# Stage edges of a two-layer decoder step on one Trainium2 core: alpha rows ordered later, meta keys in the values' tile, one PSUM division, the last beta by transfers

## The chip, the core and the metric

The kernel runs on one core of a Trainium2 chip. The metric is the device time of one execution in microseconds; of several runs the median counts. The engines are named as the profile names them: PE (TensorE, matmuls; PEld is its weight load), DVE (VectorE), ACT (ScalarE), POOL (GpSimd) and SP (SyncE, which here only issues DMAs). Each engine works through its own queue in order. DMAs issued by SP and by POOL go to the core's 16 DMA engines.

## The reference

One inference step of a decoder trunk with two layers, for a prompt of 1024 tokens behind 16 meta tokens and for 8 samples of one token with 4096 tokens of past each. Width 1024, 8 heads of 128 in layer 1, 4096 hidden units, all in float32.

```python
for layer in range(2):
    if layer == 0:
        f_p, st_p = gla_prompt(x_p, ...)          # gated linear attention in chunks of 64
        f_s, st_s = gla_sample(x_s, state_gla, ...)
    else:
        f_p, kp_rows, vp_rows = diff_prompt(x_p, ...)
        f_s, ks_rows, vs_rows = diff_sample(x_s, cache_k, cache_v, page_table, ...)
    x_p = post_norm(x_p, f_p, ln_mix_g[layer], ln_mix_b[layer])
    x_s = post_norm(x_s, f_s, ln_mix_g[layer], ln_mix_b[layer])
    x_p = post_norm(x_p, sq_relu_mlp(x_p, w1[layer], w2[layer]), ln_mlp_g[layer], ln_mlp_b[layer])
    x_s = post_norm(x_s, sq_relu_mlp(x_s, w1[layer], w2[layer]), ln_mlp_g[layer], ln_mlp_b[layer])
y_prompt = x_p[:, 16:]

def post_norm(x, f, g, b):   # DeepNorm: layer_norm(ALPHA * x + f) * g + b, ALPHA = 4 ** 0.25
    return layer_norm(ALPHA * x + f, g, b)

def diff_core(q, k, v, q_pos, k_pos, lam):
    s = einsum('bqhmd,bkhmd->bhmqk', q, k) * 64 ** -0.5   # m = 0, 1: two score maps per head
    p = softmax(where(k_pos <= q_pos, s, -inf))
    return einsum('bhqk,bkhe->bqhe', p[:, :, 0] - lam * p[:, :, 1], v)
```

The samples' attention runs over 256 pages (128 tokens, 8 heads, 128 values) of keys and as many of values, gathered by a page table: 512 KB each. The outputs are the prompt's and the samples' rows, the GLA states, and the new key and value rows of both.

## The kernel before

Weights and activations are each split into a high part and a low part, and a product is three matmuls: `mm3` (L195 to L197) multiplies high by high, high by low and low by high. `unit` loads weights in pieces (`raw`), ACT writes the high part `whi` (L182), POOL the low part `wlo` (L183). The pool `wsp` holds two buffers of each, of 2048 columns. The activations stand feature-major in `XH` and `XL`; `Y` (`Yt`, row-major, 8 tiles of 128 tokens) holds the residual stream, in which each layer's output is added up.

The stages follow each other on PE: GLA to about 480 us, its output product to 680, the MLP of layer 0 to 1436, the QKV projection to 1791, attention from 1800 to 2068, its output product (`w_out`), and from 2200 the MLP of layer 1, in 4 groups `g` of 7 up and 7 down steps `i` with operands that are sums and differences of blocks (`mlp1`, `weight_operand`, `chip_operand`). The decode of the samples (`decode`) runs beside the MLP of layer 0 and the QKV projection: SP loads pages (`pg`, L739), DVE and POOL multiply keys (L770), DVE sums (L771), PE multiplies values (L811) and turns the result (L825).

The order within an engine's queue is not written by hand throughout: a scheduler builds it from a simulated timeline, in which dependences, the buffers of pools and the banks of PSUM decide what may go when. `tc.issue_after(x)` holds the instructions written under it back behind instruction x.

- `normalize` is the LayerNorm that closes a stage: row statistics (L904, L908), the power -0.5 on POOL (L913), scale and shift on ACT, then `to_fm`, which turns the rows (PE, L930) and applies gain and shift. What the next residual needs of them is added to `Y` by `alpha_row`: L951 multiplies `Y` by the gain row times ALPHA, L953 adds the shift row times ALPHA; the rows come as tiles `ht` by DMA (L946).
- In the QKV projection, after unit u=3 `alpha_row` is written for `ln_mlp_g`, after u=6 for `ln_mlp_b`, with the four stores of the residual to `xres` (L1065). Each tile's rope is L1049 to L1052 on DVE, its stores L1058.
- Attention: `prep(h)` loads the keys and queries of a head into a tile of name `wlo` (L1101, L1102), the 16 meta tokens' keys into `km` (L1103, pool `a2`, 4 buffers, which opens once the decode pool is closed), their values into `vm`, the values into a tile of name `whi` (L1105). PE turns `km` (L1113), the keys (L1118) and the queries (L1123); POOL's DMAs move halves between partitions (L1129 to L1135), for all heads but the first. `tile_` makes scores (L1153 to L1155 for head 0, L1157 and L1158 for the others), the softmax, the transposes of the probabilities (L1176) and the product with the values (PV, L1181). `o_norm` normalises two heads at a time on POOL (L1192, L1193); `o_fm` turns the outputs for `w_out` (L1199). `prep(h + 1)` is written at the start of head h.
- PSUM has 8 banks. `psum(mm=3, ax=3, sm=2)` opens three pools; after attention `psum(mm=4, ax=2, sm=2)` closes them and opens others.
- The end: the rows of a finished tile pass `normalize`, and `last` multiplies by the gain (L1311) and adds the shift on POOL (L1314), or, for tiles 2 and 3, does both on DVE (L1319, L1320); SP stores them (L1315, L1321). `samples_out` brings the samples' sums from two PSUM banks (`acc`, filled by small products beside the weights in `beside`, L1416), turns them (L1334), normalises (`s_ln`, L470 to L491) and turns them back (L1343); before, it is written after step i=4 of the last group, whose down steps run in the order 1, 5, 6, 7, 4, 3, 2.

## Time and profile before

| | |
|---|---|
| median of 3 runs | 2927.53 us (2924.68 to 2937.85) |
| profiled execution | 2915.81 us |
| its span | 2914.1 us |
| PE busy | 2783.9 us, 96% |
| DVE busy | 1857.9 us, 64% |
| POOL busy | 1145.4 us, 39% |
| ACT busy | 1038.3 us, 36% |
| moved by DMA | 643.83 MB, mean 221 GB/s |

The span reaches from the first to the last instruction of the profiled execution; its time contains a little more. Busy times are sums over the span. PE is never short of work for long, so what is to be read is where its busy time within a stretch is below the stretch's length, where its clock is below 1.00, and what it waited for there.

### The profile page before, as it was taken

The numbers are of one execution on the slowest core, as the hardware profiler recorded it, in microseconds if no ns is written. First come the engines' busy times: TensorE is split into PE (matmuls) and PEld (weight loads), VectorE is DVE, ScalarE is ACT, GpSimd is POOL, SyncE is SP. The second block draws the span as 40 slices with busy tenths as digits, with TensorE's granted clock in tenths as the row PEclk, the third lists the DMA queues.
The fourth block names the chain that finished last, engine by engine and source line by source line (L and its number), as shares of the span: only waits on it lengthen the run. The fifth ranks groups of instructions, "written<-read, shape, count | busy, mean of one in ns | idle before, by whom it ended". The sixth has DMA issues, their size and how long they took to land. (4 is left out here: it accounts for less than half of the span.)

```text
span 2914.1 us, 52192 instructions
## 1 busy us (share of the span) xinstructions
PE 2783.9 (96%) x19668; PEld 2275.1 (78%) x19668; DVE 1857.9 (64%) x2976; ACT 1038.3 (36%) x2071; POOL 1145.4 (39%) x885
## 2 busy tenths in 40 slices
PE   8999999999999999999989999989898999999996
PEld 5776668987777777777888986878788889797985
DVE  2664544458877877777676731878438755838378
ACT  2343354151122122122411111777325535345343
POOL 1321122234333333433323430122326766677666
PEclk9999999999999999999999998999899999999998
DMA  8667541524798888988488988463427878796972
GB/s 262 210 214 248 187 168 39 191 73 164 255 341 309 309 328 310 331 315 321 137 274 288 360 298 260 102 135 84 116 98 214 230 224 234 195 288 163 270 205 86
DMA packets 299308, 643.83 MB, mean 221 GB/s; under 512 B 35168, under 2 KB 150880, under 8 KB 287792
## 3 DMA queue, kind: packets, MB, share of 16 engines
q1 hardware_dynamic: 267520, 531.15, 52.8%
q0 software_dynamic: 31536, 109.35, 15.2%
q8 instruction: 155, 2.54, 0.3%
q14 instruction: 97, 0.79, 0.1%
HBM read 582.89 MB, written 40.91 MB: 214 GB/s over the span
## 5 line engine op out<-in xcount | busy, mean ns | idle before, releaser
L183 POOL TENSOR_TENSOR wlo<-raw,whi 128x512 fp32r<-128x512 f32 x256 | 361.2, 1425 | 786.0 <-ACT whi L182 697.6
L195 PE MATMUL mmt<-whi,XH 128*128 128x256 f32 (+1 forms) x1824 | 554.0, 305 | 7.5 <-DVE qr L1051 3.8
L196 PE MATMUL mmt<-wlo,XH 128*128 128x256 f32 (+1 forms) x1824 | 550.8, 303 | 0.5 <-POOL wlo L183 0.5
L195 PE MATMUL mmt<-XH,whi 128*128 128x512 f32 (+1 forms) x1376 | 480.1, 350 | 15.7 <-DVE HL L192 6.4
L197 PE MATMUL mmt<-XH,wlo 128*128 128x512 f32 (+1 forms) x1376 | 479.4, 350 | 0.0
L197 PE MATMUL mmt<-whi,XL 128*128 128x256 f32 x1536 | 440.5, 287 | 6.8 <-DVE XL L192 6.8
L195 PEld LDWEIGHTS mmt<-whi,XH 128*128 128x128 f32 x1824 | 346.3, 190 | 43.6 <-issue 19.8
L182 ACT CAST whi<-raw 128x512 fp32r<-128x512 f32 x256 | 152.4, 619 | 619.0 <-PE mmt L197 247.3
L196 PEld LDWEIGHTS mmt<-wlo,XH 128*128 128x128 f32 x1824 | 346.6, 190 | 25.0 <-issue 11.7
L771 DVE TENSOR_REDUCE sc<-pg 128x16 f32<-128x1024 f32 x256 | 309.6, 1214 | 78.4 <-POOL pg L770 74.9
L197 PEld LDWEIGHTS mmt<-whi,XL 128*128 128x128 f32 x1536 | 292.3, 190 | 22.7 <-issue 14.8
L196 PE MATMUL mmt<-XL,whi 128*128 128x512 f32 x768 | 307.6, 400 | 0.0
L195 PEld LDWEIGHTS mmt<-XH,whi 128*128 128x128 f32 x1376 | 261.2, 190 | 57.5 <-DVE HL L192 8.2
L770 DVE TENSOR_TENSOR pg<-pg,qb 128x1024 f32<-128x1024 f32 x192 | 261.3, 1366 | 59.1 <-DMA pg<-in_cache_k 42.9
L197 PEld LDWEIGHTS mmt<-XH,wlo 128*128 128x128 f32 x1376 | 261.2, 190 | 43.6 <-issue 12.0
L770 POOL TENSOR_TENSOR pg<-pg,qb 128x1024 f32<-128x1024 f32 x64 | 156.3, 2443 | 286.3 <-DMA pg<-in_cache_k 215.0
L195 PE MATMUL mmt<-whi,HH 128*128 128x512 f32 x512 | 205.3, 401 | 1.4 <-DVE Y L995 1.4
L196 PE MATMUL mmt<-wlo,HH 128*128 128x512 f32 x512 | 204.5, 399 | 0.0
L197 PE MATMUL mmt<-whi,HL 128*128 128x512 f32 x512 | 203.7, 398 | 0.0
L196 PEld LDWEIGHTS mmt<-XL,whi 128*128 128x128 f32 x768 | 145.2, 189 | 40.4 <-issue 8.9
L196 PE MATMUL mmt<-XH,whi 128*128 128x258 f32 x608 | 173.0, 286 | 3.7 <-DMA XH<-xc 2.9
L1397 POOL TENSOR_TENSOR wlo<-RW,whi 128x512 fp32r<-128x512 f32 x96 | 152.4, 1678 | 56.6 <-ACT whi L1396 56.5
(432 smaller groups left out, 5482.1 us busy)
## 6 DMA issues: line engine op xcount, KB each, us to landing
pg<-in_cache_k SPq DMA_DIRECT2D x256, 512.0 KB
pg<-in_cache_v SPq DMA_DIRECT2D x256, 512.0 KB
XH<-xc POOLq DMA_DIRECT2D x42, 1032.0 KB, 8.8
raw<-in_mlp_w SPq DMA_DIRECT2D x164, 256.0 KB
rw<-in_mlp_w SPq DMA_DIRECT2D x156, 256.0 KB
swt<-in_mlp_w SPq DMA_DIRECT2D x32, 1024.0 KB
RW<-in_mlp_w POOLq DMA_DIRECT2D x96, 256.0 KB, 7.3
xc<-XH POOLq DMA_DIRECT2D x14, 1032.0 KB, 8.0
```

Of the source, the lines that this page charges most:

```text
L182: S.copy(hi[:, c], raw)
L183: G.tensor_tensor(lo[:, c], raw, hi[:, c].bitcast(F32), op=ALU.subtract)
L195: TE.matmul(ps, ah, bh, start=first, stop=False)
L196: TE.matmul(ps, ah, bl, start=False, stop=False)
L197: TE.matmul(ps, al, bh, start=False, stop=last)
L770: eng.tensor_tensor(pg, pg, qb, op=ALU.mult)
L771: return V.tensor_reduce(sc[:, n, :], pg.rearrange("p (h d) -> p h d", d=64), op=ALU.add, axis=AX.X).ins
L1397: G.tensor_tensor(lo[:, k, :], t, hi[:, k, :].bitcast(F32), op=ALU.subtract)
```

## The change

Five edits, in the order of the program.

1. The three PSUM pools are opened once, with 3, 3 and 2 banks, and stay. The tiles of `mlp1` take a bank of `ax` at every other tile instead of every third.
2. The `alpha_row`s of layer 0's second norm are held behind the last step of DVE that the program has recorded so far (`steps_v[-1]`): the rope of the unit they are written after. Their loads and the stores to `xres` follow them.
3. `km` is no tile of its own; the meta tokens' keys lie in columns 1024 to 1151 of the values' tile `whi`.
4. The last norm's shift is written into `y_prompt` beforehand, by one transfer from DRAM to DRAM that repeats the row `ln_mlp_b[1]` 1024 times; the finished rows, with the gain alone, are added to it by POOL's accumulating transfers. For tiles 2 and 3 ACT multiplies by the row's scale. Only the gain row is held on the chip.
5. In the last group, the samples' loads that stood beside four operands (i=5, 6, 7, 4) all stand beside two (i=5 and 6), and `samples_out` is written after i=6.

```diff
-    psum(mm=3, ax=3, sm=2)
+    mm = ctx.enter_context(tc.tile_pool(name="mm", bufs=3, space=PSUM))
+    ax = ctx.enter_context(tc.tile_pool(name="ax", bufs=3, space=PSUM))
+    sm = ctx.enter_context(tc.tile_pool(name="sm", bufs=2, space=PSUM))
...
         if u == 3:
-            list(alpha_row(A["ln_mlp_g"][0:1], ALU.mult))
+            with tc.issue_after(steps_v[-1]):
+                list(alpha_row(A["ln_mlp_g"][0:1], ALU.mult))
         elif u == 6:
-            for j in alpha_row(A["ln_mlp_b"][0:1], ALU.add):
-                cs = slice(256 * j, 256 * j + 256)
-                dma(A["xres"][:, cs].rearrange("(t p) n -> p t n", p=P), Yt[:, :, cs])
+            with tc.issue_after(steps_v[-1]):
+                for j in alpha_row(A["ln_mlp_b"][0:1], ALU.add):
+                    cs = slice(256 * j, 256 * j + 256)
+                    dma(A["xres"][:, cs].rearrange("(t p) n -> p t n", p=P), Yt[:, :, cs])
...
-        km, vm = a2.tile([NM, P], F32, name="km"), vms[h % 2]
+        km, vm = vk[:NM, 1024 : 1024 + P], vms[h % 2]
...
-    psum(mm=4, ax=2, sm=2)
...
-    fgb = [XF[1][:, 1024 * i : 1024 * (i + 1)] for i in range(2)]
+    fg = XF[1][:, :1024]
...
-        y = Yt[:, t, :]
+        y, out = Yt[:, t, :], A["y_prompt"][0, t * P : (t + 1) * P, :]
         if t not in (2, 3):
-            V.tensor_tensor(y, y, fgb[0], op=ALU.mult)
-            for h in range(4):
-                c = slice(256 * h, 256 * h + 256)
-                G.tensor_tensor(y[:, c], y[:, c], fgb[1][:, c], op=ALU.add)
-            dma(A["y_prompt"][0, t * P : (t + 1) * P, :], y)
+            V.tensor_tensor(y, y, fg, op=ALU.mult)
+            nc.gpsimd.dma_start(out, y, accum_op=ALU.add)
             return
         for h in range(2):
             c = slice(512 * h, 512 * h + 512)
-            V.scalar_tensor_tensor(y[:, c], y[:, c], mv[:, t, 0:1], fgb[0][:, c], ALU.subtract, ALU.mult)
-            V.scalar_tensor_tensor(y[:, c], y[:, c], rs[:, 0, t : t + 1], fgb[1][:, c], ALU.mult, ALU.add)
-            dma(A["y_prompt"][0, t * P : (t + 1) * P, c], y[:, c])
+            V.scalar_tensor_tensor(y[:, c], y[:, c], mv[:, t, 0:1], fg[:, c], ALU.subtract, ALU.mult)
+            S.activation(y[:, c], y[:, c], AF.Copy, scale=rs[:, 0, t : t + 1])
+            nc.gpsimd.dma_start(out[:, c], y[:, c], accum_op=ALU.add)
...
-        beside.quarter = {5: (0, 0), 6: (1, 1), 7: (0, 1), 4: (1, 0)}.get(i)
+        quarters = {5: [(0, 0), (1, 0)], 6: [(0, 1), (1, 1)]} if g == 3 else {5: [(0, 0)], 6: [(1, 1)], 7: [(0, 1)], 4: [(1, 0)]}
...
-                down_tile(g, i, t, *now, axt() if n % 3 == 0 else mmt())
+                down_tile(g, i, t, *now, axt() if n % 2 else mmt())
...
-            if g == 3 and not up and i == 4:
+            if g == 3 and not up and i == 6:
                 samples_out()
...
-                for x, nm in zip(fgb, "gb"):
-                    dma(x, A["ln_mlp_" + nm][1:2].broadcast_to([P, D]))
+                dma(fg, A["ln_mlp_g"][1:2].broadcast_to([P, D]))
+                dma(A["y_prompt"][0], A["ln_mlp_b"][1:2].broadcast_to([T, D]))
```

What the scheduler makes of it is seen in the queues. The lines of the changed kernel are 7 to 9 lower than those of the kernel before (L811 is L802 there, L1113 is L1106, L1153 is L1146, L1176 is L1169, L1181 is L1174, L1199 is L1192, L195 is L186).

PE's queue at the start of attention, before: `pg` are the last pages of values, `km` and `wlo` the first heads' meta keys, keys and queries, `XH_83` and `XL_85` head 0's operands.

```order
L197 MATMUL mmt<-whi,XL_86 128x256
L811 MATMUL smt<-pg,sc 16x256 x12
L825 MATMUL smt<-c_ident,pg 128x128 x2
L1113 MATMUL axt<-c_ident,km 128x16
L1118 MATMUL axt<-c_ident,wlo 128x128 x4
L1123 MATMUL axt<-c_ident,wlo 128x128 x4
L1118 MATMUL axt<-c_ident,wlo 128x128 x4
L1123 MATMUL axt<-c_ident,wlo 128x128 x4
L1113 MATMUL axt<-c_ident,km 128x16
L1153 MATMUL mmt<-XH_83 128x352
L1154 MATMUL mmt<-XL_85,XH_83 128x352
L1153 MATMUL mmt<-XH_83 128x352
```

The same place in the changed kernel; the meta keys are read from `whi`:

```order
L188 MATMUL mmt<-whi,XL_86 128x256
L1106 MATMUL axt<-c_ident,whi 128x16
L1111 MATMUL axt<-c_ident,wlo 128x128 x4
L802 MATMUL smt<-pg,sc 16x256 x4
L1116 MATMUL axt<-c_ident,wlo 128x128 x4
L802 MATMUL smt<-pg,sc 16x256 x4
L1111 MATMUL axt<-c_ident,wlo 128x128 x4
L802 MATMUL smt<-pg,sc 16x256 x4
L1116 MATMUL axt<-c_ident,wlo 128x128 x4
L802 MATMUL smt<-pg,sc 16x256 x4
L1146 MATMUL mmt<-XH_83 128x352
L1147 MATMUL mmt<-XL_85,XH_83 128x352
```

The preparation of head 0 moved in front of the last pages, between single ones, and so did head 0's first score products; 16 more page matmuls, head 1's preparation and the last 32 page matmuls follow them.

PE's queue within a head in the middle of attention, before (`XH_83`, `XL_85`: the operands of the head whose scores are made; `vm_21001` and `whi` behind L1181: the values of the head before it; `km` and `wlo`: the next head's rows):

```order
L1157 MATMUL mmt<-XH_83 128x384
L1158 MATMUL mmt<-XH_83,XL_85 128x384
L1176 MATMUL axt<-c_ident,as 128x128 x4
L1113 MATMUL axt<-c_ident,km 128x16
L1118 MATMUL axt<-c_ident,wlo 128x128 x4
L1157 MATMUL mmt<-XH_83 128x400
L1158 MATMUL mmt<-XH_83,XL_85 128x400
L1157 MATMUL mmt<-XH_83 128x384
L1158 MATMUL mmt<-XH_83,XL_85 128x384
L1181 MATMUL smt<-vm_21001,aT 128x128
L1181 MATMUL smt<-whi,aT 128x128 x3
L1123 MATMUL axt<-c_ident,wlo 128x128 x4
```

The same head in the changed kernel:

```order
L1174 MATMUL smt<-vm_21001,aT 128x128
L1174 MATMUL smt<-whi,aT 128x128 x3
L1150 MATMUL mmt<-XH_83 128x384
L1151 MATMUL mmt<-XH_83,XL_85 128x384
L1150 MATMUL mmt<-XH_83 128x400
L1151 MATMUL mmt<-XH_83,XL_85 128x400
L1150 MATMUL mmt<-XH_83 128x384
L1151 MATMUL mmt<-XH_83,XL_85 128x384
L1106 MATMUL axt<-c_ident,whi 128x16
L1111 MATMUL axt<-c_ident,wlo 128x128 x4
L1116 MATMUL axt<-c_ident,wlo 128x128 x4
```

The transpose of the meta keys moved from two score pairs ahead of the last PV products to three score pairs behind them.

PE's queue at the end of attention, before; `Y` holds the heads' outputs, `XH_83` and `XL_85` now their feature-major parts, and L195 to L197 are `w_out`:

```order
L1199 MATMUL axt<-c_ident,Y 128x128 x4
L1181 MATMUL smt<-vm_21001,aT 128x128
L1181 MATMUL smt<-whi,aT 128x128 x3
L1199 MATMUL axt<-c_ident,Y 128x128 x4
L1181 MATMUL smt<-whi,aT 128x128 x2
L1199 MATMUL axt<-c_ident,Y 128x128 x24
L1285 MATMUL smt<-zoq,one 128x64
L195 MATMUL mmt<-whi,XH_83 128x256
L196 MATMUL mmt<-wlo,XH_83 128x256
```

The changed kernel where its first product of `w_out` stands; behind the last row shown, further ones stand among the last heads' L1169 and L1174:

```order
L1192 MATMUL axt<-c_ident,Y 128x128 x4
L1150 MATMUL mmt<-XH_84 128x336
L1151 MATMUL mmt<-XH_84,XL_86 128x336
L1150 MATMUL mmt<-XH_84 128x320
L1151 MATMUL mmt<-XH_84,XL_86 128x320
L1192 MATMUL axt<-c_ident,Y 128x128 x4
L186 MATMUL mmt<-whi,XH_83 128x256
L187 MATMUL mmt<-wlo,XH_83 128x256
L188 MATMUL mmt<-whi,XL_85 128x256
L186 MATMUL mmt<-whi,XH_83 128x256
```

The first products of `w_out` moved from behind attention's last transpose to a place ahead of the last head's PV products.

## Rows read from the trace of the kernel before

**Rows 1.** the page: busy us, share of the span, instructions:
```profile
PE 2783.9 (96%) x19668; PEld 2275.1 (78%) x19668; DVE 1857.9 (64%) x2976; ACT 1038.3 (36%) x2071; POOL 1145.4 (39%) x885
```

**Rows 2.** windows: stretch, length; busy PE, PEld, DVE, ACT, POOL; PEclk, DMA share, GB/s:
```profile
0.00:20.00 20.00, 10.99 (x55) 8.14 (x56) 9.30 (x19) 8.56 (x15) 2.70 (x6) 1.00 0.94 326
1440.00:1500.00 60.00, 49.36 (x388) 45.65 (x389) 48.06 (x64) 16.35 (x26) 11.48 (x8) 0.89 0.69 219
1500.00:1520.00 20.00, 20.00 (x184) 18.49 (x183) 9.14 (x17) 4.58 (x8) 7.51 (x5) 1.00 1.05 395
1500.00:1780.00 280.00, 277.14 (x2554) 245.13 (x2555) 148.47 (x214) 48.33 (x88) 87.47 (x57) 0.99 0.92 324
1780.00:1830.00 50.00, 43.19 (x255) 33.43 (x256) 18.98 (x58) 16.66 (x37) 6.11 (x11) 0.66 0.68 178
2040.00:2080.00 40.00, 30.03 (x201) 26.00 (x200) 26.98 (x67) 27.04 (x53) 14.87 (x11) 0.84 0.44 137
```

**Rows 3.** timeline at the end (start, duration, engine; in brackets the wait before):
```profile
2894.31 0.40 PE L197 MATMUL axt<-whi,XH 128*128 128x512 f32 x1
2907.74 0.59 PE L1343 MATMUL smt<-c_ident,sx 128*32 128x128 f32 x2 [13.03 <-DVE sx L491]
2895.74 1.40 DVE L1319 SCALAR_TENSOR_TENSOR Y<-Y,bmv,XR 128x512 f32<-128x512 f32 x2
2910.64 0.33 SPq L1321 DMA_DIRECT2D out_y_prompt<-Y  x1
```

**Rows 4.** TensorE's longest waits, whole span: total us, times, longest:
```profile
PE mmt L1157 <- DMA XH<-XH: 8.0, 4, 2.8
PE axt L1199 <- DVE Y L1193: 4.4, 2, 3.4
PE smt L280 <- DMA swt<-in_gla_w_in: 4.1, 1, 4.1
```

**Rows 5.** timeline of VectorE and TensorE at 1447 us, and the residual's stores:
```profile
1447.35 1.23 DVE L951 SCALAR_TENSOR_TENSOR Y<-Y,ht 128x1024 f32<-128x1024 f32 x1 [6.10 <-DMA ht<-in_ln_mlp_g]
1452.17 0.35 PE L195 MATMUL mmt<-whi,XH 128*128 128x256 f32 x1 [2.66 <-DVE qr L1051]
L1065 SPq DMA_DIRECT2D xres<-Y x4: 359/377/382, 1473.3 to 1491.1; - x4
```

**Rows 6.** groups of VectorE's instructions by line, 1440 to 1500 us:
```profile
L951 DVE SCALAR_TENSOR_TENSOR Y<-Y,ht 128x1024 f32<-128x1024 f32 x8 | 11.3, 1436 | 6.1 <-DMA ht<-in_ln_mlp_g 6.1
L953 DVE SCALAR_TENSOR_TENSOR Y<-ht,Y 128x1024 f32<-128x1024 f32 x8 | 10.4, 1354 | 4.8 <-DMA ht<-in_ln_mlp_b 4.8
```

**Rows 7.** timeline at attention's start: SP's issues, TensorE:
```profile
1793.54 2.99 SPq L1103 DMA_DIRECT2D km<-out_k_rows_p  x4
1799.42 0.26 PE L1113 MATMUL axt<-c_ident,km 16*128 16x16 f32 x1 [4.30 <-DMA km<-out_k_rows_p]
```

**Rows 8.** timeline between two heads: TensorE, SP, POOL:
```profile
1881.32 0.23 PE L1113 MATMUL axt<-c_ident,km 16*128 16x16 f32 x1
1882.90 0.83 PE L1181 MATMUL smt<-whi,aT 128*128 128x128 f32 x6
1903.13 0.69 PE L1157 MATMUL mmt<-XH 128*128 128x352 f32 x2 [2.82 <-DMA XH<-XH]
1883.77 0.38 SPq L1105 DMA_DIRECT2D whi<-out_v_rows_p  x1
1893.30 2.94 POOL L1192 TENSOR_TENSOR orr<-orr,mhalf 128x16 f32<-128x16 f32 x1
1902.96 3.62 POOL L1193 TENSOR_TENSOR Y<-Y,orr 128x2048 f32<-128x2048 f32 x1
```

**Rows 9.** groups of POOL's instructions by line, 2800 us to the end:
```profile
L1314 POOL TENSOR_TENSOR Y<-Y,XR 128x256 f32<-128x256 f32 x24 | 22.9, 985 | 5.7 <-DVE Y L1311 5.7
L1395 POOL DMA_DIRECT2D RW<-in_mlp_w x8 | 8.3, 1512 | 0.0
```

**Rows 10.** the page: accumulating transfers of 256 KB, median us to landing:
```profile
RW<-in_mlp_w POOLq DMA_DIRECT2D x96, 256.0 KB, 7.3
```

More of the change, by code (lines that the diff above doesn't have):

```diff
@@ L121, in hybrid_step @@
     wrp = ctx.enter_context(tc.tile_pool(name="wrp", bufs=2))
[L122 to L133 removed]
+    mm = ctx.enter_context(tc.tile_pool(name="mm", bufs=3, space=PSUM))
+    ax = ctx.enter_context(tc.tile_pool(name="ax", bufs=3, space=PSUM))
+    sm = ctx.enter_context(tc.tile_pool(name="sm", bufs=2, space=PSUM))
     def mmt():
[L136 removed]
+        return mm.tile([P, 512], F32, name="mmt")
     def axt():
[L139 removed]
+        return ax.tile([P, 512], F32, name="axt")
     def smt():
[L142 removed]
+        return sm.tile([P, 512], F32, name="smt")
     def cload(name, pool=cp):
@@ L1375, in chip_operand, with weight_operand @@
         return hi, lo
-    def weight_operand(terms, quarter, side=None):
+    def weight_operand(terms, quarter, side=None, beside=None):
         hi, lo = (wsp.tile([P, 2048], F32R, name=n).rearrange("p (k n) -> p k n", n=512) for n in ("whi", "wlo"))
@@ L1397, in weight_operand @@
             G.tensor_tensor(lo[:, k, :], t, hi[:, k, :].bitcast(F32), op=ALU.subtract)
-            if side:
+            for q in side or ():
                 t = rawt()
-                dma(t, src(side.quarter, k))
-                side(k, t)
+                dma(t, src(q, k))
+                beside(k, t, *q)
         return hi, lo
@@ L1503, in mlp1 @@
                         n += 1
[L1504 removed]
+                        up_tile(g, i, t, c, *now, axt() if n % 2 else mmt())
                     continue
                 n += 1
[L1507 removed]
+                down_tile(g, i, t, *now, axt() if n % 2 else mmt())
                 if g == 3:
```

19 lines of the change are left out of this document (3 added, 16 removed).

## The prediction

> **What bounds the kernel now.** I read the page's totals first: TensorE is busy for 2783.9 us, 96% of the span of 2914.1 us [rows 1], so the kernel is TensorE's work, and a change that leaves the matmuls alone can win only where TensorE is idle or runs at its lower clock. The second view is the table of windows [rows 2]; next to each busy time stand the count of matmuls, the granted clock and the share of the DMA engines. Three stage edges stand out. From 1440 to 1500 us, where the QKV projection starts, 388 matmuls took 60 us; the 20 us behind them hold 184 of the same kind, by which 388 need 388 / 9.2 = 42.2 us: 17.8 us lost. From 1780 to 1830, into attention, TensorE is busy for 43.19 of 50 us at a mean clock of 0.66, so about 43.19 x 0.66 = 28.5 us of work at the full clock: 21.5 lost. From 2040 to 2080, out of attention, 30.03 x 0.84 = 25.2 of 40: 14.8 lost. A fourth edge is the end: the last product starts at 2894.31 [rows 3] and the span ends at 2914.1. The third view is TensorE's longest waits [rows 4]: beside one of 13.03 us at the very end, for the samples' norm [rows 3], 8.0 us in four waits for attention's moves between heads, 4.1 us for a weight tile in the first 40 us.
>
> The sum is made in microseconds of the profiled execution, whose own time is 2915.81; the median of the three timed runs is 2927.53, 11.7 us above it, and I add the sum to the median.
>
> **The change part by part.**
>
> *Alpha rows moved.* At 1447 VectorE stands for 6.10 us before the first L951, for a row of gains that a DMA brings, and TensorE then waits 2.66 us for rope results queued behind it on VectorE [rows 5]. The 16 instructions L951 and L953 hold VectorE for 11.3 + 10.4 = 21.7 us and its queue for 6.1 + 4.8 us more [rows 6]. In the new order VectorE goes straight to rope, splits and pages; the 16 stand some 80 to 190 instructions later, into a stretch (1500 to 1780) in which TensorE is busy for 277.14 of 280 us and VectorE for 148.47 [rows 2], so there TensorE's own work covers them; without that cover they would cost their 21.7 us again. What can come back on TensorE is 0 to 17.8 us. But the decode pages run in the same stretch. Their stream had a DMA share of 0.69 where 1.05 is seen next door [rows 2], so 60 x 0.36 / 1.05 = 20.6 us of stream stood unused. SP's queue moves too: the four stores of the residual (L1065, 1024x256 floats to each 1 MB) lay in that slack, from 1473.3 to 1491.1 [rows 5], and now go out in the full stretch, where 4.19 MB at 395 GB/s are 10.6 us of stream. So at best 20.6 - 10.6 = 10 us of pages are won. I take -9, bounds 0 and -16.
>
> *Meta keys in the values' tile, first head.* The loads L1103 were issued at 1793.54, when the decode pool's memory came free; the transposes L1113 waited 4.30 us for them, and with them the whole preparation of head 0 [rows 7]. In the new order the preparation stands between the last page matmuls L811, and the first score products before the last 48 of them. The loss of 21.5 us shrinks by what fits there; it does not vanish, since decode's stream must still end and the first softmax must still run. I take -12, bounds -3 and -20; the clock is part of this, since the matmuls from 1800 on are those after the gap.
>
> *The same, heads 2 to 7.* Here the edit adds a wait. The keys of head h+1 now go where the values of head h-1 lie, and those are read until that head's last PV product (L1181). Before, L1113 ran at 1881.32, ahead of the last PV, which starts at 1882.90; the values' own load was issued at 1883.77, right behind it [rows 8]. Now the keys' load stands where the values' load stood, and L1113, which is in TensorE's queue ahead of L1118 and L1123, comes behind it. In the new order that is two pairs of L1157/L1158 and the last PV later than before, some 2.3 us. Queued behind it are eight L1118/L1123 transposes each for keys and queries, then the moves on POOL, and the next head's first score, which already waited 2.82 us for a move at 1903.13 [rows 8] and 8.0 us in all at four heads [rows 4]: these four starts are bound by this chain, so every microsecond counts in full: 4 x 2.3 = 9.2, and about 1 for the two that had slack. I take +10. It is 0 if the order's model is right that the keys land in time and the pairs cover them, and +20 if two of POOL's own rows come in front of the moves: L1192 (2.94 us) and L1193 (3.62 us) now stand ahead of moves which they used to follow [rows 8].
>
> *PSUM division kept.* Closing and opening the pools after attention kept the products of w_out behind attention's last transposes. Now 3/3/2 banks last throughout, and w_out's products L195 to L197 stand among the last L1199, L1176 and L1181. They need no new data but the first heads' outputs, and fill the waits of that stretch, whose worst is 3.4 us for L1193 [rows 4]. Of the 14.8 us lost I take -8, bounds -2 and -13. In the MLP the tiles alternate between 3 and 3 banks where it was 4 and 2; a wait for a bank does not show among TensorE's waits, so I put it at 0.
>
> *Beta by transfers.* The output is pre-filled with beta by one transfer from DRAM to DRAM of 4.19 MB that depends on nothing and stands early in SP's queue, ahead of weight loads. At 326 GB/s with a share of 0.94 [rows 2] it is 12.9 us of all DMA engines. TensorE waited 4.1 us for a weight tile there [rows 4]. The new order puts some 56 other matmuls of 512 columns in front of that product; those of 256 run at 9.2 a us [rows 2], so 56 / 4.6 = 12 us of cover. I take +1, bounds -4 and +12.
>
> *The end.* 24 additions L1314, 22.9 us of POOL, go [rows 9], and with them what they put off on POOL, the weights' low halves L1397 among it. Four L1320 become ScalarE copies. The samples' last norm now comes in step 6 instead of step 4 of the last group, ahead of the last products, so the wait of 13.03 us at 2907.74 [rows 3] goes. What then ends is the chain of the last tile: the add L1468, statistics, the power on POOL, L1319 with 2 x 0.70 [rows 3], a copy and the issue; eight short steps, for which I put 6 us, as an estimate from L1319's size and the gaps between engines, and then the store. A plain one took from 2910.64 to the end, 3.5 us [rows 3]; the nearest row of an accumulating one is 7.3 us in the median, under load [rows 10]. So the tail is 9.5 to 13.3 us where it was 19.4. Against that, the samples' 16 weight tiles now all come in two steps. I take -10, bounds -2 and -16.
>
> The 10 stores also leave SP for POOL, whose DMA issues took 1512 ns in the mean in this stage [rows 9]. On such issues the Trainium skill ("SBUF — State Buffer", section "SBUF: two separate sides") says that GpSimd writes the descriptors of its transfers through a port pair which VectorE can lock, so that a DMA of about 620 ns took about 3100 beside a VectorE copy. By that rule the last store would end 2.5 us later and the sum would be -25.5 instead of -28; whether the 1512 ns of an issue have this cause no run here shows.
>
> The sum: -9 - 12 + 10 - 8 + 1 - 10 = -28 us, 2927.5 - 28 = **2899.5 us**.
>
> **The rivals.**
>
> *The head chain costs what the edges give.* Each odd head pays 2.3 + 2.94 + 3.62 = 8.9 us, each even one 2.3: 3 x 8.9 + 3 x 2.3 = 33.6 in place of 10. Then the sum is -4 and the time 2923. For it speaks POOL's new order, against it that L1192 has its input early and may run in a gap. Chance 0.15.
>
> *The stream of pages gives nothing back.* Slack is not used, because pages wait for their buffers and not for VectorE; the two first edges together give 4 instead of 21. Sum -11, time 2916. Chance 0.10.
>
> *Slower: decode ends later.* The place is 1500 to 1780 us, where the DMA share is 0.92, and 1.05 at its start. If the page stream is what ends last there, the residual's 10.6 us lie in front of it, and if page products on VectorE are its limit, the 21.7 us of alpha rows too: +32 where I have -21. Sum +25, time 2952. It decides from +23 on these two edges upward against the other terms' -7, and the time passes 2942. Against it speaks VectorE's 148.47 of 280. Chance 0.12.
>
> *The end does not shrink.* The accumulating stores take their 7.3 us and the samples' loads starve the last operands: 0 for -10, time 2909. This is the case in which that part of the change doesn't do what it says. Chance 0.08.
>
> **How the numbers follow.** The forecast has 0.55; its own range is 2880 to 2912. A measurement of this kernel tells about 0.5%, 14.6 us, from no change, so faster means below 2912.9, slower above 2942.1. The forecast and the flat end make faster 0.63; the head chain and the idle stream make 0.25 the same; decode ending later makes 0.12. The range has to hold 8 in 10: upward it takes in the two cases of no change and the bound of the start, 2936; downward, with edges nearer to their bounds, 2870.
>
> **What would show it.** Of the changed kernel I look for: 1440 to 1500 with over 480 matmuls and no wait of VectorE for the gains' rows; attention's first scores before 1795 and a clock of 1.00 from 1810 on; L1113 behind the last PV, and heads that start 2 to 3 us further apart than before; w_out's products before the last transposes and no window below 17 of 20 there; a last product that is followed by 9 to 14 us. The prediction is wrong if the head period grows by 5 us or more, if attention's first scores come no earlier than 1800, or if TensorE waits over 8 us for weights in the first 140 us.

## The result and the profile after

The changed kernel takes 2942.7 us in the median of 11 runs (2932.9 to 2949.1), the kernel before 2927.4 us of 11 (2922.0 to 2937.9): ratio 1.0048, 95% interval 1.0031 to 1.0064, 15 us slower where 28 faster was forecast. Single executions of one kernel differ by some 10 us here, and the two profiled ones lie at opposite ends (2949.14 against 2915.81), so each kernel was profiled a second time (*a_again* 2936.95, *b_again* 2927.18); times by stage are taken from that pair unless said otherwise. One of the six executions of *b_fill* below took 13280 us at a granted clock of 0.191; its ratio goes by the other five.

From the page of the changed kernel, the span and TensorE's totals; they answer to [rows 1]:

```profile
span 2946.3 us, 52168 instructions
PE 2789.4 (95%) x19668; PEld 2274.8 (77%) x19668; DVE 1858.8 (63%) x2972; ACT 1038.9 (35%) x2072; POOL 1123.3 (38%) x871
```

The work is the same 19668 matmuls; the time is in the idle stretches. Windows of the changed kernel at the places of [rows 2] (stretch, length; busy PE, PEld, DVE, ACT, POOL; granted clock, DMA share, GB/s):

```profile
20.00:40.00 20.00, 20.00 (x105) 10.87 (x104) 6.80 (x12) 4.21 (x8) 2.54 (x2) 1.00 0.81 150
40.00:60.00 20.00, 8.82 (x40) 6.49 (x42) 0.00 (x0) 0.60 (x1) 0.00 (x0) 0.78 1.01 246
1474.00:1534.00 60.00, 58.18 (x515) 54.61 (x514) 35.62 (x64) 19.82 (x33) 19.00 (x13) 1.00 0.78 252
1814.00:1864.00 50.00, 39.41 (x275) 29.15 (x272) 21.91 (x73) 18.45 (x44) 6.32 (x13) 0.76 0.74 199
2083.00:2123.00 40.00, 38.16 (x317) 36.77 (x318) 24.41 (x57) 23.70 (x45) 8.92 (x8) 1.00 0.33 106
2926.90:2946.30 19.40, 0.00 (x0) 0.00 (x0) 8.00 (x15) 5.50 (x7) 7.17 (x9) 0.63 0.74 123
```

Two of the four edges closed as forecast: 515 matmuls in the 60 us at the QKV start (388 before), 38.16 us busy of 40 out of attention (30.03). Attention's start and the end did not, and a new hole stands in the second 20 us of the kernel, where TensorE is busy for 8.82 us. What TensorE waits for is in the timeline of SP and TensorE there, with TensorE's row at the same tile in the kernel before:

```profile
32.12 0.67 SPq L1505 DMA_DIRECT2D out_y_prompt<-in_ln_mlp_b  x1
32.90 0.57 SPq L214 DMA_DIRECT2D swt<-in_gla_w_in  x1
59.34 1.08 PE L271 MATMUL smt<-swt,sx 128*32 128x512 f32 x4 [11.18 <-DMA swt<-in_gla_w_in]
```
```profile
38.98 1.19 PE L280 MATMUL smt<-swt,sx 128*32 128x512 f32 x8 [4.09 <-DMA swt<-in_gla_w_in]
```

The early transfer goes out 0.8 us ahead of a weight tile's load, and TensorE waits 11.18 us for such a tile, where it was 4.1 [rows 4]. The wait is only a part of what the first stage loses. TensorE up to the first add of layer 0's MLP, in *a_again* and, second, in *b_again*:

```profile
0.00:679.60 679.60, 627.03 (x5479) 487.74 (x5480) 313.20 (x649) 245.26 (x550) 153.19 (x106) 0.97 0.54 176
```
```profile
0.00:651.80 651.80, 616.93 (x5479) 481.39 (x5480) 319.66 (x649) 249.11 (x553) 151.61 (x106) 0.99 0.54 177
```

TensorE is idle there for 52.6 us instead of 34.9, and busy for 10.1 us more at a mean clock of 0.97 instead of 0.99.

A ledger by stage, each entry the stage's length less its length in *b_again* (us; a stage ends at the first or last row of the named line; line numbers of before). But for rounding, every column adds up to the difference of the spans:

| stage, up to | a_again | a_fill_quiet | p_psum | p_alpha | p_km |
|---|---|---|---|---|---|
| first add of layer 0's MLP, L995 | +27.8 | +4.8 | +1.8 | +5.8 | +4.3 |
| first rope of QKV, L1049 | -3.4 | -3.4 | +0.6 | -0.7 | +0.6 |
| last page product, L811 | +12.2 | +8.0 | +0.4 | +8.1 | -1.5 |
| first softmax, L1161 | -13.6 | -13.6 | -2.1 | -6.4 | -8.7 |
| last PV, L1181 | +5.2 | +3.3 | -11.9 | -1.9 | +0.5 |
| w_out's end, L930 | -22.0 | -22.0 | -22.0 | +0.1 | 0.0 |
| last product, L197 | +5.0 | +6.4 | -1.5 | -2.7 | -4.7 |
| end of span | -1.5 | -2.8 | +0.3 | -0.1 | -0.1 |
| sum | +9.8 | -19.3 | -34.4 | +2.3 | -9.5 |

Entries up to some 6 us stand also where a kernel changes nothing in a stage (the first line of p_alpha; the heads, L1161 to L1181, are 7 us shorter in the first trace of before than in b_again), so one entry is read as a size only above that, and the timed ratios decide.

### The profile page after: what moved, and what is told of

It reads as the page before. It is cut to its first block, busy times and chain, and to the rows that moved or that the text cites. A ratio compares the mean times of both kernels' runs of the same rounds, so it can differ in the third digit from the quotient of the medians.

```text
span 2946.3 us, 52168 instructions
## 1 busy us (share of the span) xinstructions
PE 2789.4 (95%) x19668; PEld 2274.8 (77%) x19668; DVE 1858.8 (63%) x2972; ACT 1038.9 (35%) x2072; POOL 1123.3 (38%) x871
## 5 line engine op out<-in xcount | busy, mean ns | idle before, releaser
L186 PE MATMUL mmt<-whi,XH 128*128 128x256 f32 (+1 forms) x1760 | 526.1, 301 | 4.7 <-DVE qr L1042 2.0
L187 PE MATMUL mmt<-wlo,XH 128*128 128x256 f32 (+1 forms) x1760 | 524.9, 299 | 0.9 <-POOL wlo L174 0.9
L186 PE MATMUL mmt<-XH,whi 128*128 128x512 f32 (+1 forms) x1216 | 438.4, 361 | 9.5 <-DVE HL L183 6.7
L188 PE MATMUL mmt<-XH,wlo 128*128 128x512 f32 (+1 forms) x1216 | 436.7, 360 | 0.0
L188 PE MATMUL mmt<-whi,XL 128*128 128x256 f32 x1536 | 434.1, 284 | 1.8 <-DVE XL L183 1.8
L186 PEld LDWEIGHTS mmt<-whi,XH 128*128 128x128 f32 x1760 | 331.4, 189 | 34.6 <-issue 20.0
L187 PEld LDWEIGHTS mmt<-wlo,XH 128*128 128x128 f32 x1760 | 332.8, 189 | 29.1 <-issue 17.6
L186 PEld LDWEIGHTS mmt<-XH,whi 128*128 128x128 f32 x1216 | 233.0, 192 | 49.6 <-DVE HL L183 8.1
L188 PEld LDWEIGHTS mmt<-XH,wlo 128*128 128x128 f32 x1216 | 232.8, 192 | 38.8 <-issue 6.3
L186 PE MATMUL mmt<-whi,HH 128*128 128x512 f32 x512 | 205.3, 401 | 1.4 <-DVE Y L986 1.4
L1387 POOL TENSOR_TENSOR wlo<-rw,whi 128x512 fp32r<-128x512 f32 x92 | 142.2, 1626 | 37.8 <-ACT whi L1386 32.7
```

The lines of the kernel that those rows point to most:

```text
L186: TE.matmul(ps, ah, bh, start=first, stop=False)
L187: TE.matmul(ps, ah, bl, start=False, stop=False)
L188: TE.matmul(ps, al, bh, start=False, stop=last)
L1387: G.tensor_tensor(lo[:, k, :], t, hi[:, k, :].bitcast(F32), op=ALU.subtract)
```

## The experiments

*The same two kernels again,* for a second trace of each.

> The changed kernel once more, for a second trace: the profiled execution of the changed kernel was the longest of its eleven, that of before shorter than its ten others. What differs between executions of one kernel must show here. Theory A: the MLP of layer 0 starts 30 us or more later than in before's trace in this one too. Theory B: it starts within 10 us of before's.

> The kernel before once more, for a second trace. If the GLA stage's length is a matter of the order and not of the execution, the MLP of layer 0 starts at 652 us within 4 us; what varies by 10 us between executions should be seen at one stage.

Measured: 2936.95 and 2927.18 us. The first stage is 27.8 us longer again (first traces: 33.7), so the hole is no accident of one execution: theory A, though by less than its 30 us.

**The early transfer.** Alone in the kernel before (*b_fill*, first diff); in the changed kernel, held until the loads of layer 0's residual, about 500 us (*a_fill_late*), or until w_out's last weight load, about 2150 us (*a_fill_quiet*, second diff). In b_fill and the kernels with fewer rows the output is written a second time at the end as before.

```diff
+                dma(A["y_prompt"][0], A["ln_mlp_b"][1:2].broadcast_to([T, D]))
```
```diff
+    with tc.issue_after(loads[-1]):
+        dma(A["y_prompt"][0], A["ln_mlp_b"][1:2].broadcast_to([T, D]))
...
-                dma(A["y_prompt"][0], A["ln_mlp_b"][1:2].broadcast_to([T, D]))
```

> The kernel before with one thing added: the transfer that writes the last norm's shift row into the prompt's output, from DRAM to DRAM, at the place in the program where the change has it; the additions on POOL and the plain stores stay, so the output is written a second time by them. Theory A, the early transfer makes the GLA stage later by some 30 us (waits for weight tiles and an order of the GLA stage that the scheduler built around it): 25 to 35 us above the kernel before, about 2955 us, and in its trace the MLP of layer 0 starts at about 685 us where before had 652. Theory B, the transfer hides and the loss of the changed kernel lies behind 1440 us (decode, attention): within 5 us of the kernel before.

> The changed kernel with that transfer held behind the residual's loads at the end of the GLA stage (about 500 us), all else as changed. Theory A: 25 to 35 us below the changed kernel, 2908 to 2918 us, so 10 to 20 us faster than before, and the MLP of layer 0 starts at about 652 us again. Theory B: within 5 us of the changed kernel, about 2940 us.

> The changed kernel with the full transfer held behind the last weight load of attention's output product, near 2150 us, where the DMA engines were a third busy. Theory A, what the transfer costs depends on the weights behind it in the queue, and there it is free: 24 to 28 us below the changed kernel, about 2915 us, some 9 us faster than before, and the MLP of layer 0 starts at about 653 us. Theory B, 4.19 MB cost 12 us of all DMA engines wherever they stand, as in the kernel that held it to 500 us: about 2926 us, the same as before.

Measured: b_fill 2948.0, ratio 1.0084 (1.0057 to 1.0110); a_fill_late 2926.5, 1.0006 (0.9987 to 1.0025); a_fill_quiet 2910.4, 0.9955 (0.9939 to 0.9970). The transfer alone costs more than the whole change (25 us, the low end of theory A). Moved to 500 us it still costs 0.5% against a_fill_quiet, where neither theory had it: the MLP of layer 0 starts 12.8 us later than there. With the transfer at 2150 us the changed kernel is faster than before. In b_fill VectorE runs the first stage in the changed kernel's order, in a_fill_quiet in that of the kernel before; so these runs price the transfer together with the order that comes with it.

**Bytes or order?** A scheduler orders the first stage, and makes another order for each size of transfer. Transfers of 32, 128, 256, 512 and 960 rows, alone in the kernel before, each with an order of its own (*b_small, b_128, b_256, b_512, b_960*):

```diff
+                dma(A["y_prompt"][0, :128], A["ln_mlp_b"][1:2].broadcast_to([128, D]))
```

> The kernel before with an early transfer of the shift row into 32 output rows (131 KB) instead of 1024 (4.19 MB), at the same place of SP's queue; nothing else changed. The GLA stage's order is again another than before's, since the scheduler answers to the transfer. Theory A, it is the 4.19 MB in front of the weight tiles that cost the 24 us: within 5 us of before, and TensorE's wait for the weight tile near 40 us stays at about 4 us. Theory B, any other order of the GLA stage loses, whatever the transfer's size: 10 to 25 us slower.

> The kernel before with an early transfer of 128 output rows (0.52 MB) of the shift ahead of the weights, and nothing else; these rows are written again at the end, so the output is the same. The 32-row transfer (0.13 MB) cost 0.60%, the whole 4.19 MB 0.84%. Theory that an early transfer costs by the order of the first stage that the scheduler makes with it: this one has another order than both, so the time may lie anywhere between 1.000 and 1.008, with the MLP's first add of layer 0 at 652 us where it is 1.000 and 663 where it is 1.006. Rival, that any transfer ahead of the first weights costs some 15 us whatever the order: 1.006 again, with TensorE waiting for a weight tile in the first 60 us longer than 4 us.

> The kernel before with an early transfer of 256 output rows (1.05 MB), nothing else. So far 0.13 MB cost 0.60%, 0.52 MB 0.07%, 4.19 MB 0.84%, each with another order of the first stage. Theory that the order decides: the cost does not follow the bytes, and with this order and the two beside it lies anywhere from 0 to 25 us. Rival, that the bytes decide for large transfers: 1.05 MB take about 3 us of all DMA engines at 326 GB/s, so at most a fourth of the whole one's 24 us, 6 us or 0.2%.

> The same with 512 rows (2.10 MB). Order decides: anywhere from 0 to 25 us, not between its neighbours. Bytes decide: about half of the whole transfer's 24 us, 10 to 14 us, 0.4%, and the wait for the third weight tile of the samples' product in the first 60 us between 4 and 9 us.

> The same with 960 rows (3.93 MB), 15/16 of the whole transfer's bytes, with a third order. Bytes decide: 0.75 to 0.85%, 22 to 25 us, with a wait of about 9 us for the weight tile at 50 to 70 us. Order decides: clearly off that, under 0.5%, at the same wait for the tile.

| | MB | ratio, 95% | wait for the weight tile | last samples' product L280, later by |
|---|---|---|---|---|
| b_small | 0.13 | 1.0060, 1.0044 to 1.0075 | 3.0 | 1.0 |
| b_128 | 0.52 | 1.0007, 0.9989 to 1.0025 | 3.4 | 0.6 |
| b_256 | 1.05 | 1.0026, 1.0011 to 1.0041 | 3.3 | 1.0 |
| b_512 | 2.10 | 1.0050, 1.0035 to 1.0065 | 5.8 | 6.0 |
| b_960 | 3.93 | 1.0100, 1.0082 to 1.0117 | 9.5 | 15.2 |
| b_fill | 4.19 | 1.0084, 1.0057 to 1.0110 | 9.2 | 15.0 |

The row behind the longest wait, from TensorE's timeline of b_960 and, second, of b_512:

```profile
56.39 1.94 PE L280 MATMUL smt<-swt,sx 128*32 128x512 f32 x8 [9.46 <-DMA swt<-in_gla_w_in]
```
```profile
47.23 1.94 PE L280 MATMUL smt<-swt,sx 128*32 128x512 f32 x8 [5.76 <-DMA swt<-in_gla_w_in]
```

From 1.05 MB on the timed cost grows with the bytes, 8, 15, 29 and 25 us, some 6 to 7 us per MB (0.52 MB: 2 us), and from 2.10 MB on so do the wait and the delay of the last samples' product; a rival by which the order alone decides does not give that. But b_small costs 0.60% with a transfer that delays nothing there (wait 3.0 us, less than before's 4.1), while four times the bytes in another order cost nothing that can be told. In the traces VectorE, ScalarE and GpSimd run b_small, b_128 and b_512 in one and the same order from the first add of layer 0's MLP on, so what sets b_small apart should lie in the first stage. Its one trace, of the fastest of its six executions, has that stage only 3.5 us longer than b_128's. That an order alone can cost some 15 us is thus argued from the timed ratios, not seen in a trace, and a share of the order in the cost of b_960 and b_fill is not excluded.

By their traces only these two stand clear: up to the first add they are 29.0 and 27.6 us longer than b_again, b_small, b_128, b_256 and b_512 11.5, 8.0, 13.1 and 8.5, and kernels in which VectorE keeps before's order in this stage up to 8.8 (q_end).

**PSUM division alone** (*p_psum*; two lines of six, the diff at the head of the document has the rest):

```diff
-    psum(mm=4, ax=2, sm=2)
...
-                        up_tile(g, i, t, c, *now, axt() if n % 3 == 0 else mmt())
+                        up_tile(g, i, t, c, *now, axt() if n % 2 else mmt())
```

> The kernel before with the PSUM part alone: 3, 3 and 2 banks throughout, every other tile of the last MLP in the second pool. The traces of the changed kernel have 22 us less from attention's last PV product to the last transpose of its output stage. Theory A, that gain is of this part: 18 to 24 us below before, about 2904 us, with w_out's products among attention's last rows. Theory B, it comes from the shorter preparation or the other orders of the changed kernel, or the last MLP pays it back with 3 and 3 banks: within 8 us of before.

Measured: 2907.8 us, 0.9955 (0.9938 to 0.9972). Windows out of attention, of p_psum and, second, of b_again, and between them TensorE's first product of w_out in p_psum:

```profile
2040.00:2080.00 40.00, 38.39 (x324) 37.14 (x324) 21.51 (x48) 19.09 (x36) 7.52 (x6) 1.00 0.42 136
```
```profile
2044.62 0.36 PE L186 MATMUL mmt<-whi,XH 128*128 128x256 f32 x1 [0.57 <-DVE ast L1152]
```
```profile
2046.00:2086.00 40.00, 28.67 (x196) 24.24 (x194) 27.55 (x63) 26.65 (x50) 14.63 (x11) 0.88 0.43 132
```

The first product of w_out stands 20 us ahead of the last PV (2064.7), the clock stays at 1.00, and 324 matmuls run where 196 did. The ledger's -22 counts from the last PV and so credits work that was done before it (76 of w_out's matmuls, about 8 us); 22 - 8 = 14 us agrees with the timed 13 (8 to 18). Its place is theory A's, its size less than the 18 to 24 us expected.

**Alpha rows alone** (*p_alpha*) **and meta keys alone** (*p_km*):

```diff
+            with tc.issue_after(steps_v[-1]):
+                list(alpha_row(A["ln_mlp_g"][0:1], ALU.mult))
```
```diff
-        km, vm = a2.tile([NM, P], F32, name="km"), vms[h % 2]
+        km, vm = vk[:NM, 1024 : 1024 + P], vms[h % 2]
```

> The kernel before with the alpha rows of layer 0's second norm held back, alone. In the changed kernel's traces the projection's first rope comes 4 us earlier against the MLP's end, but the last page's product 14 us later against the last rope. Theory A, the rows and the residual's stores in the full stream make decode end later: the first gain stays at 4, the last page product L811 comes 10 to 16 us later than in before, and the kernel is 5 to 12 us slower, about 2934 us. Theory B, decode ends later because of where head 0's preparation stands (the meta keys' part): L811 is not later here, and the kernel is 2 to 6 us faster, about 2921 us.

> The kernel before with the meta keys in the values' tile, alone. Theory A (decode's end belongs to the alpha rows): the first scores come some 30 us ahead of the last page product, the first softmax 10 to 14 us earlier than in before, and the head chain gives back 8 to 10 us by the last PV: 0 to 6 us faster, about 2922 us. Theory B (decode's end belongs to this part): the last page product 10 to 15 us later, the first softmax where it was, and the heads 8 to 10 us longer: 8 to 14 us slower, about 2936 us.

Measured: 2924.6, 1.0009 (0.9992 to 1.0026), and 2922.8, 1.0007 (0.9989 to 1.0025). Windows of p_alpha, the QKV start and the decode stretch, and, second, the start in b_again:

```profile
1448.00:1508.00 60.00, 59.66 (x530) 56.46 (x530) 37.70 (x66) 19.92 (x33) 19.94 (x14) 1.00 0.77 257
1500.00:1780.00 280.00, 270.46 (x2457) 241.98 (x2456) 162.95 (x219) 45.74 (x83) 82.55 (x52) 0.99 0.90 312
```
```profile
1439.00:1499.00 60.00, 48.64 (x387) 45.26 (x388) 48.09 (x65) 16.20 (x26) 12.41 (x9) 0.89 0.70 218
```

The start gains 143 matmuls, some 15 us of TensorE's time at 9.2 a us [rows 2]. From 1500 to 1780 TensorE is then busy for 270.46 us instead of 277.14 [rows 2], and the last page product comes 129.2 us behind the last rope instead of 120.0. TensorE's longest wait of the stretch from 1500 to 1808 us (total us, times, longest), in p_alpha and, second, the same line in b_again:

```profile
PE smt L811 <- DMA pg<-in_cache_v: 15.4, 11, 5.9
```
```profile
PE smt L811 <- DMA pg<-in_cache_v: 2.4, 2, 1.8
```

The matmuls now wait for pages: what they gained at the start they lose where the stream of pages ends last. Decode's end moves as theory A had it, by somewhat less; the time is neither theory's. The meta keys' edit brings the first softmax 8.7 us nearer to the last page product, but six distances between heads add up to 195.4 us in p_km, 199.6 and 197.3 in the changed kernel's traces, and 182.9 and 189 in before's: 6 to 17 us more. Over all traces the two groups do not overlap: 195.3 to 199.6 us in the six with the meta keys moved, 180.6 to 191.1 in the fourteen without, 13 us more in the mean. The ledger's +0.5 for p_km from the first softmax to the last PV lies within the scatter of that stage (before's own two traces differ by 7.5 there). In time p_km is neutral. Its last page product stays where it was, as theory A had it; its first softmax gains less than theory A's 10 to 14 us, and its first scores come 3 us behind the last page product, not 30 ahead. One such boundary of the changed kernel (second trace; TensorE, SP, POOL), to be read against [rows 8]:

```profile
1968.12 0.83 PE L1174 MATMUL smt<-whi,aT 128*128 128x128 f32 x6
1970.63 0.20 PE L1106 MATMUL axt<-c_ident,whi 16*128 16x16 f32 x1
1968.99 0.33 SPq L1096 DMA_DIRECT2D whi<-out_k_rows_p  x1
1977.22 2.94 POOL L1185 TENSOR_TENSOR orr<-orr,mhalf 128x16 f32<-128x16 f32 x1
1982.58 3.63 POOL L1186 TENSOR_TENSOR Y<-Y,orr 128x2048 f32<-128x2048 f32 x1
1987.22 0.56 POOL L1128 DMA_DIRECT2D XH<-XH  x1 [1.02 <-DMA XH<-XH]
1990.72 0.52 POOL L1128 DMA_DIRECT2D XL<-XL  x1 [2.94 <-DMA XL<-XL]
```

The keys are loaded and transposed (L1106, before L1113) behind the last PV of the head that held the tile, and POOL's two long rows stand in front of the moves L1128. This boundary, the fifth, takes 40 to 41 us in the changed kernel's two traces where others take 29 to 34; in a_fill_quiet it takes 35.4, in p_km 32.8.

**Samples' loads and norm alone** (*p_samples*; the shift is still added on chip):

```diff
+        quarters = {5: [(0, 0), (1, 0)], 6: [(0, 1), (1, 1)]} if g == 3 else {5: [(0, 0)], 6: [(1, 1)], 7: [(0, 1)], 4: [(1, 0)]}
...
-            if g == 3 and not up and i == 4:
+            if g == 3 and not up and i == 6:
```

> The kernel before with the samples' loads beside two operands of the last group instead of four and their norm after step 6, alone; shift rows still added on the chip, plain stores. Theory A, the changed kernel's end stayed at 19 us because of its accumulating stores: here the end behind the last product shrinks to 10 to 12 us and the kernel is 5 to 9 us faster, about 2918 us. Theory B, the 16 weight tiles in two steps starve the operands ahead of it and give the gain back: the last product comes 5 to 8 us later and the kernel stays within 4 us of before.

Measured: 2929.7, 1.0015 (0.9997 to 1.0034). POOL's timeline at its end:

```profile
2893.84 15.33 POOL L1314 TENSOR_TENSOR Y<-Y,XR 128x256 f32<-128x256 f32 x16 [2.57 <-DVE brs L917]
2909.13 1.58 POOL L913 TENSOR_TENSOR brs<-brs,mhalf 128x1 f32<-128x1 f32 x3
```

With the samples' wait gone, the last powers L913 wait behind 15.33 us of POOL's additions, which is what the shift by transfers takes away. From the last product to the end 23.5 us pass, 2.7 more than in b_again, which neither theory had. The shift by transfers was not run alone. Both edits together win nothing over the PSUM division either, as long as every tile is stored by accumulating: q_end below has 0.9951, p_psum 0.9955.

**The end.** *q_end* leaves alpha rows and meta keys as before and fills at 2150 us; *q_mix* lets only tiles 4 to 7 be stored by accumulating; *q_mix2* tiles 0, 1 and 4 to 7, with plain stores for 2 and 3, which come last; *a_mix2* is q_mix2 with alpha rows and meta keys as changed. The diff is q_mix's; in q_mix2 the line with t >= 4 is gone, and with it the additions on POOL (tiles 2 and 3 get their shift on VectorE, as before, not on POOL as the expectation has it).

```diff
         if t not in (2, 3):
             V.tensor_tensor(y, y, fgb[0], op=ALU.mult)
+            if t >= 4:
+                nc.gpsimd.dma_start(A["y_prompt"][0, t * P : (t + 1) * P, :], y, accum_op=ALU.add)
+                return
```

> The kernel before with the PSUM part, the samples' part and the shift row by transfers, the early transfer held to near 2150 us; the alpha rows and the meta keys stay as before. Theory A, the accumulating stores are what ends last: all 1024 of their packets take twice the time of a plain store's, so the end behind the last product stays at 19 to 21 us, and the kernel is as the PSUM part alone, 2905 to 2910 us. Theory B, the end shrinks by 6 to 10 us once the early transfer is out of the way: about 2900 us.

> As q_end, but only tiles 4 to 7, which are finished some 30 us before the end, are stored by accumulating transfers (and only their rows are written beforehand); tiles 0 to 3 get their shift row on the chip and plain stores as before. Theory A (accumulating stores are slow, but hidden when they come early; POOL's 16 fewer additions free the last products and the last rows): the end behind the last product is 10 to 14 us, the kernel 6 to 9 us faster than the PSUM part alone, about 2900 us, and the fastest of all. Theory B (the end is bound by VectorE's rows of the last four tiles): no better than q_end.

> PSUM division, samples' norm and the shift by transfers, alpha rows and meta keys as before; the last group's tiles 0, 1 and 4 to 7 get their shift by accumulating stores onto an output filled late, tiles 2 and 3 get it on POOL and a plain store. Theory that POOL's additions of tiles 0 to 3 stand ahead of a statistics power at the end: with half of them gone POOL's 8.3 us row in front of the last power is gone too, about 4 us less than the kernel with four tiles on chip, ratio 0.991 to before, under 16 us behind the last product. Rival, that the accumulating stores of the last two tiles end the kernel by themselves: the same time as that kernel, 0.993, or 1 to 3 us more, as the two more accumulating stores cost.

> The kernel above with alpha rows held and meta keys in the values' tile as in the changed kernel. Theory that these two edits together give back at the stage edges what they take in decode and between heads: within 0.2% of the kernel above. Rival, that they lose: the heads' 10 us and the decode end's 9 against the 4 us of the QKV start and the earlier first scores leave +6 to +10 us, 0.2 to 0.35% over the kernel above.

| | us | ratio to before, 95% | last product to the end |
|---|---|---|---|
| q_end | 2909.2 | 0.9951, 0.9932 to 0.9970 | 20.3 |
| q_mix | 2903.2 | 0.9930, 0.9915 to 0.9945 | 17.4 |
| q_mix2 | 2907.9 | 0.9940, 0.9918 to 0.9962 | 14.8 |
| a_mix2 | 2901.5 | 0.9926, 0.9908 to 0.9944 | 14.4 |

POOL and VectorE at the end of q_mix, and, second, SP's last store in q_mix2:

```profile
2899.74 8.27 POOL L1311 TENSOR_TENSOR Y<-Y,XR 128x256 f32<-128x256 f32 x8 [2.28 <-DVE Y L1305]
2907.97 1.06 POOL L906 TENSOR_TENSOR brs<-brs,mhalf 128x1 f32<-128x1 f32 x2
2908.55 2.74 DVE L1317 SCALAR_TENSOR_TENSOR Y<-Y,brs,XR 128x512 f32<-128x512 f32 x4 [1.12 <-POOL brs L906]
```
```profile
2895.05 3.71 SPq L1313 DMA_DIRECT2D out_y_prompt<-Y  x4
```

Taking the 8.27 us from in front of the power shortens the end by 2.6 us more, less than the 4 expected; between the totals of the last three kernels their intervals do not tell. In q_mix2 the last store, a plain one, is issued by 2898.8 us, 3.3 us ahead of the end; in the changed kernel 7.4 us pass behind an accumulating one (below). Alpha rows and meta keys on top of q_mix2 cost nothing that can be told. a_mix2 is the fastest median, 0.74% or 22 us below before.

## Why the prediction was wrong

**The early transfer: the step that failed.** It was put at +1, at most +12; it costs 25 us alone (b_fill), and taking it to a quiet place gives the changed kernel 0.9% back (1.0048 to 0.9955). A wait of over 8 us for weights in the first 140 us was named as a sign of being wrong, and it came. Two parts of the step were wrong. The transfer was priced at 12.9 us of the DMA engines from the 326 GB/s of the first 20 us; in the changed kernel it competes with the loads issued behind it, and from 40 to 60 us the share is 1.01 at 246 GB/s. The product that needs the tile starts at 59.34 us instead of 38.98, 20.4 us later. And the 12 us of matmuls put in front did not cover it, for the wait was 11.18 us in spite of them. Nor is the wait, some 7 us more than before, the whole: the last samples' product comes 15.6 us later in a_again, the states' products L413 26.8, and of TensorE's 17.7 us of additional idle time in a_again's first stage 5.7 are this wait (9.9 us against 4.2). The step priced nothing behind that product; how the rest divides between late loads and the new order stays open. The loss stood outside the bound given.

**Alpha rows: right at the edge, wrong for the whole.** The window shows what was forecast, 515 matmuls, no wait of VectorE for the gains' row. But I took the decode stretch as covered by TensorE's work, and dismissed the slower rival, that the page stream ends last, by VectorE's 148 of 280 us. That rival's mechanism was right in part: alone, the edit moves decode's end by 8.1 us and is neutral in time (1.0009) instead of -9.

**Meta keys.** First head -12 forecast: from the last page product to the first softmax 13.6 us less, in the changed kernel. Heads 2 to 7 +10 forecast: +8 to +17 by the head distances, 13 in the mean of all traces. Both sizes were about right, but the last page product comes 12.2 us later, so -13.6 and +12.2 are to be read together. For pages TensorE waits 4.2 us in all here; its longest wait is another one, 6.83 us, which the prediction did not have. TensorE and VectorE at attention's start in the changed kernel:

```profile
1815.30 0.42 PE L1146 MATMUL mmt<-XH 64*128 64x352 f32 x1
1827.21 0.33 DVE L1074 MEMSET cmask<- 128x320 f32 x1 [11.24 <-SPq L728]
1827.46 1.30 DVE L183 TENSOR_TENSOR XL<-axt,XH 128x16 fp32r<-128x16 f32 x3
1827.62 1.12 PE L1111 MATMUL axt<-c_ident,wlo 128*128 128x128 f32 x4 [6.83 <-DVE XL L183]
1829.52 5.37 PE L802 MATMUL smt<-pg,sc 128*16 128x256 f32 x64
1836.64 0.41 PE L816 MATMUL smt<-c_ident,pg 128*128 128x128 f32 x2 [1.75 <-ACT pg L813]
```

The first scores (L1146) stand 19.6 us ahead of the end of the last page products, as the order said. But the transposes of head 1's keys (L1111) stand in TensorE's queue ahead of the last page products (L802). They wait for low halves on VectorE (L183), and these stand behind the memset of the mask, before which VectorE was idle for 11.24 us until SP had come to decode's last page numbers (L728). So decode's end waits for a preparation that itself waits for decode's loads. The same wait is 7.2 us in a_again and 7.8 in a_fill_quiet, and p_alpha and p_km do not have it: only kernels with both edits do. The window is still 39.41 of 50 us at clock 0.76. In a_fill_quiet, without the first stage's delay, the first scores come at 1780.1 us (before: 1804.0) and the clock is 0.75 from 1810 to 1820, then 1.00; scores before 1795 were forecast rightly, a clock of 1.00 from 1810 on was not.

**PSUM division: right, mis-sized.** -8 (bound -13) forecast, 13 us measured alone; nearly the whole 14.8 us of that window came back, and no cost of the 3 and 3 banks in the MLP can be told from the executions' scatter.

**The end: wrong.** -10 forecast; 19.4 us from the last product to the end in the first traces of both, 19.3 against 20.8 in the second. The samples' wait went as forecast, 13.03 us [rows 3] to 0.61, but the chain and the store each took more. The changed kernel's end (TensorE, then VectorE, POOL, ScalarE):

```profile
2922.34 0.92 PE L1333 MATMUL smt<-c_ident,sx 128*32 128x128 f32 x7 [0.61 <-DVE sx L482]
2929.91 1.21 DVE L1304 TENSOR_TENSOR Y<-Y,XR 128x1024 f32<-128x1024 f32 x1
2931.03 0.68 DVE L1458 TENSOR_TENSOR Y<-Y,mmt 128x512 f32<-128x512 f32 x1
2932.41 1.41 DVE L1309 SCALAR_TENSOR_TENSOR Y<-Y,bmv,XR 128x512 f32<-128x512 f32 x2
2934.04 1.40 DVE L1309 SCALAR_TENSOR_TENSOR Y<-Y,bmv,XR 128x512 f32<-128x512 f32 x2
2936.15 1.33 ACT L1310 ACTIVATE Y<-Y,brs 128x512 f32<-128x512 f32 x2 [1.20 <-POOL brs L904]
2937.17 1.76 POOL L1311 DMA_DIRECT2D out_y_prompt<-Y  x2 [0.19 <-issue]
```

The last store is issued by 2937.17 + 1.76 = 2938.9, 12.0 us behind the last product, where I put 6: the chain was priced for one tile, but VectorE has four tiles' last steps in its queue there, with L1304 of another tile ahead of the last add L1458. From there to the end 7.4 us pass, where a plain store took 3.5: the accumulating store's 7.3 [rows 10] was the right row. The feared blocking of POOL's issues did not show: they take 0.88 us each (1.76 for two), below the 1512 ns mean of [rows 9].

Of the forecast's -28, then: +24 us too little for the transfer, 9 too much gain for the alpha rows, 9 for the end, 5 too little for the PSUM division, and the rest in the meta keys and scatter: 24 + 9 + 9 - 5 = 37 of the 43 us between 2899.5 and 2942.7.

## What to carry to other kernels

A transfer that depends on nothing is not free because it is early: ahead of the first weights, from one megabyte on, each cost here 6 to 7 us with the order that came with it, twice its time on the DMA engines (12.9 us for 4.19 MB), and the same transfer in a stretch with idle DMA engines cost nothing that could be told. A stage edge that is closed gives time only if the stage behind it is bound by the engine that won; where a stream of loads ends last, the matmuls wait there instead. Two edits that are neutral alone can meet in one queue and make a wait that neither has. And before an operation at the very end is exchanged for a transfer, price the whole queue behind the last product, for all its tiles, and the store of the new kind from a row of that kind.

## What the runs showed of the hardware

Accumulating stores to DRAM are slower per packet than plain ones: in the trace of the changed kernel's end their 4096-byte packets take 328 ns in the median, plain stores' 160 and 161 ns in the two traces of before. It is not POOL's queue by itself: POOL's plain stores of `xc` to DRAM (L1364) from 2206 to 2226 us take 329 ns for packets of 8256 bytes, about as long per byte as the plain stores. Between partitions POOL's plain moves are as slow as the accumulating stores: 326 ns for 4096 bytes from 1830 to 2060 us. The last windows show it: a DMA share of 0.74 at 123 GB/s in the changed kernel (above), and in the last 20.4 us of b_again:

```profile
2905.00:2925.40 20.40, 1.86 (x8) 1.01 (x8) 15.36 (x32) 4.09 (x6) 12.03 (x14) 0.61 0.34 130
```

About twice the DMA engines' time for the same bytes a second. By the view of DMA issues, the accumulating stores land 5.6 and 5.7 us after their issue in the median:

```profile
out_y_prompt<-Y POOLq DMA_DIRECT2D x6, 512.0 KB, 5.6
out_y_prompt<-Y POOLq DMA_DIRECT2D x4, 256.0 KB, 5.7
```

And b_small's 15 us, which its 3.0 us of waiting for the weight tile do not explain, are timed and not traced: the order of the first stage is the reading that is left, not one that was run by itself.
